# Matmul with layer norm: B loaded in half-width blocks that three row panels share, late gamma and beta, and a last panel computed quarter by quarter

## The chip, the cores and the metric

The kernel runs on one core of one Trainium2 chip. The metric is the device time of one execution in microseconds (us). The profile's span, from the first to the last instruction, is about 2 us shorter than the time. The *granted clock* is the share of PE's full clock that the profile shows as allowed.

Engines are called as the profile calls them: PE (matrix engine; "PEld" its weight loads), DVE (vector engine), ACT (scalar engine), POOL and SP (here they mostly issue transfers).

## The reference

```python
m, k, n = 2048, 2048, 2048          # a: m x k, b: k x n, all float32
x = np.matmul(a, b)
mean = np.mean(x, axis=-1, keepdims=True)
var = np.var(x, axis=-1, keepdims=True)
out = gamma * (x - mean) / np.sqrt(var + eps) + beta
```

The kernel computes the product in float16 with float32 sums. The cast happens in the load.

## The kernel before

The 2048 rows of A are 16 *panels* of 128 rows. A panel is loaded whole (1 MiB read), transposed by PE in 16 pieces (two groups of eight, each copied out of PSUM by ACT), and multiplied with the 16 row blocks of B (128 rows each, index `kt`). One panel's result is four *quarters* of 128 x 512, and each quarter fills one PSUM bank. Seven banks serve quarters, one serves transposes. A quarter takes 16 matmuls. Then DVE takes its statistics (`bn_stats`), ACT copies it to SBUF, and the bank is free. When all four are done, DVE makes two elementwise passes per quarter, and SP stores the panel.

```python
a16_lst[0] = emit_a_load(0)
a16_lst[1] = emit_a_load(1)
for kt in range(n_kt):                                   # B: 16 transfers of 1 MiB
    nc.gpsimd.dma_start(b16[:, kt, :], b[ts(kt, P), :])
at_lst[0] = emit_transposes(a16_lst[0], 0)
nc.sync.dma_start(gamma_b, gamma.unsqueeze(0).to_broadcast([P, N]))
nc.sync.dma_start(beta_b, beta.unsqueeze(0).to_broadcast([P, N]))
# ... [cut]
for i in range(n_mt):
    alloc_panel(i)                                       # four banks of seven
    for kt in range(n_kt):
        for q in range(n_nb):
            emit_mm(i, q, kt)
        if kt == n_kt // 2 - 1:
            # [cut] transposes of panel i+1, load of panel i+2
    x_sb_l[i] = [quarter_done(i, q) for q in range(n_nb)]   # bn_stats, copy
    emit_ln(i)                                              # 2 passes x 4 on DVE, stores
```

A scheduler reorders instructions at build time and the order on each engine is then fixed. It had moved three of panel 1's quarters up into panel 0, so that all seven banks were in use while B arrived.

## Time and profile before

| | |
|---|---|
| time | 284.34 us (4 runs, 284.25 to 284.39) |
| span of the profiled run | 282.4 us |
| first transpose | 10.3 us |
| B complete in PE's eyes | 53.2 us |
| last matmul ends | 270.7 us |
| PE busy | 87% of the span |

The timeline of PE before. Columns: start, duration, engine, source line, operation, output<-inputs, number of instructions, and in brackets the idle time before it with what ended it.

```profile
10.29 1.03 PE L76 MATMUL tps<-ident,a 128*128 128x128 f16 x8 [10.29 <-DMA a<-in_a_dram]
...
22.69 1.67 PE L107 MATMUL cps<-b,at 128*128 128x512 f16 x7 [0.85 <-DMA b<-in_b_dram]
...
53.20 1.67 PE L107 MATMUL cps<-b,at 128*128 128x512 f16 x7 [0.77 <-DMA b<-in_b_dram]
...
250.80 19.91 PE L107 MATMUL cps<-b,at 128*128 128x512 f16 x91
```

Seven matmuls (tps are transposes, cps quarters), a wait for B, seven matmuls: PE follows the loads until 53.2 us. After 64 us it has no listed gap, so it is the limit. The last line starts at 250.80 and lasts 19.91 us, so the last matmul ends at 270.71.

The waits of PE before (who waited for whom, us in total, times, longest):

```profile
PE cps L107 <- DMA b<-in_b_dram: 13.3, 15, 1.9
...
PE tps L76 <- DMA a<-in_a_dram: 11.0, 2, 10.3
```

The end of the chain of waits before, which follows the work that ended last (start, us, what; DVEq is DVE's sequencer):

```profile
250.97 19.12 PE cps L107 x88
270.08 0.02 issue
270.11 2.50 DVE bnst L116 x4
...
277.79 0.66 DVEq L189
```

Four bn_stats stand in the tail, then eight elementwise passes.

### The profile page before, as it was taken

How to read it: one execution, taken by the hardware profiler on the slowest of the kernel's cores; microseconds unless marked ns; L12 is line 12 of the kernel's file. 1: busy time of each engine (PE TensorE's matmuls, PEld its weight loads, DVE VectorE, ACT ScalarE, POOL GpSimd, SP SyncE). 2: the span in 40 equal slices, each digit the busy share in tenths (PEclk: the TensorE clock that was granted, in tenths of full speed). 3: DMA queues.
4: the chain of work that ended last, by engine and by line, in shares of the span. 5: the costliest groups of instructions: out<-in, count | busy, mean ns of one | idle time of the engine just before them, and what ended most of it. 6: DMA issues, size and time to landing. Idle time of an engine off the chain costs nothing.

```text
span 282.4 us, 3151 instructions
## 1 busy us (share of the span) xinstructions
PE 244.6 (87%) x1280; PEld 115.6 (41%) x1280; DVE 132.5 (47%) x241; ACT 73.9 (26%) x114; POOL 17.7 (6%) x38
## 2 busy tenths in 40 slices
PE   0286666699999999999999999999999999999930
PEld 0242222244444454545454545444444545454410
DVE  0000000389390919283645647382909092836474
ACT  1230000254232323232323232222323232323030
POOL 7122120000000000000000000000000000000000
PEclk9999999999999999999999999999999999999995
DMA  7999999967616160605243343425161203030303
GB/s 268 241 211 214 214 214 213 214 102 256 161 75 149 68 158 13 193 20 178 48 157 66 151 74 138 85 89 136 74 149 68 84 13 138 0 149 2 149 0 149
DMA packets 9517, 35.84 MB, mean 127 GB/s; under 512 B 1056, under 2 KB 1056, under 8 KB 9248
## 3 DMA queue, kind: packets, MB, share of 16 engines
q0 software_dynamic: 4608, 16.78, 31.6%
q1 hardware_dynamic: 4896, 18.88, 16.9%
q8 instruction: 10, 0.16, 0.2%
q14 instruction: 3, 0.02, 0.0%
HBM read 35.65 MB, written 16.78 MB: 186 GB/s over the span
## 4 chain that ended last, share of the span: by engine, by line
PE 73%; DMA 18%; DVE 5%; ACT 2%; issue 1%; POOL 0%; DVEq 0%; POOLq 0%
PE cps L107 68%; DMA b<-in_b_dram 14%; PE tps L76 5%; DMA a<-in_a_dram 4%; DVE c L139 2%; DVE u L135 2%; DVE bnst L116 1%; ACT x L118 1%; ACT L127 0%; DVEq L189 0%; POOL a L67 0%; DVE mv L123 0%; POOL ident masks.py:199 0%; ACT sq L127 0%; POOL ident masks.py:197 0%
## 5 line engine op out<-in xcount | busy, mean ns | idle before, releaser
L107 PE MATMUL cps<-b,at 128*128 128x512 f16 x1024 | 231.4, 380 | 13.6 <-DMA b<-in_b_dram 13.3
L107 PEld LDWEIGHTS <-at 128*128 128x128 f16 x1024 | 99.0, 98 | 131.7 <-issue 22.1
L116 DVE BATCH_NORM_STATS2 bnst<-cps 128x6 f32<-128x512 f32 x64 | 39.9, 685 | 143.1 <-PE cps L107 143.1
L118 ACT COPY x<-cps 128x512 f32<-128x512 f32 x64 | 37.4, 585 | 113.2 <-DVE bnst L116 112.3
L77 ACT COPY at<-tps 128x1024 f16<-128x1024 f16 x32 | 32.4, 1011 | 85.4 <-PE tps L76 85.4
L135 DVE SCALAR_TENSOR_TENSOR u<-x,mv,gamma_b 128x512 f32<-128x512 f32 x64 | 46.0, 742 | 0.0
L139 DVE SCALAR_TENSOR_TENSOR c<-u,rstd,beta_b 128x512 f32<-128x512 f32 x64 | 45.1, 745 | 0.0
L76 PE MATMUL tps<-ident,a 128*128 128x128 f16 x256 | 20.9, 227 | 12.6 <-DMA a<-in_a_dram 11.0
L76 PEld LDWEIGHTS <-a 128*128 128x128 f16 x256 | 17.9, 102 | 22.9 <-DMA a<-in_a_dram 11.5
L67 POOL DMA_DIRECT2D a<-in_a_dram x16 | 8.6, 538 | 166.4 <-PE tps L76 159.0
L86 POOL DMA_DIRECT2D b<-in_b_dram x16 | 8.5, 541 | 22.0 <-DMA b<-in_b_dram 15.5
L123 DVE BATCH_NORM_AGGREGATE mv<-bnst 128x2 f32<-128x24 f32 x16 | 4.2, 264 | 0.6
L127 ACT ACTIVATE sq<-ve 128x1 f32<-128x1 f32 x16 | 3.3, 207 | 0.0
L129 DVE RECIPROCAL rstd<-sq 128x1 f32<-128x1 f32 x16 | 2.5, 156 | 1.0 <-ACT sq L127 1.0
L125 DVE TENSOR_TENSOR ve<-mv,eps_t 128x1 f32<-128x1 f32 x16 | 2.5, 159 | 0.5
L77 ACT ACT_TABLE_LOAD x1 | 1.3, 1283 | 0.7 <-PEq L175 0.7
L127 ACT ACT_TABLE_LOAD x1 | 1.3, 1283 | 0.0
L93 DVE MEMSET eps_t<- 128x1 f32 x1 | 0.1, 59 | 0.8 <-PEq L175 0.8
masks.py:199 POOL TENSOR_SCALAR_AFFINE_SELECT ident<-ident 128x128 f16<-128x128 f16 x1 | 0.3, 304 | 0.1
masks.py:197 POOL MEMSET ident<- 128x128 f16 x1 | 0.2, 204 | 0.3 <-POOLq L175 0.3
L175 POOL MEMSET const-float32-0.0<- 128x1 f32 x1 | 0.1, 98 | 0.2 <-issue 0.2
L175 POOL MEMSET const-bfloat16-1.0<- 128x1 bf16 x1 | 0.1, 101 | 0.0
(2 smaller groups left out, 0.2 us busy)
## 6 DMA issues: line engine op xcount, KB each, us to landing
out_dram<-c SPq DMA_DIRECT2D x32, 512.0 KB, 2.6
a<-in_a_dram POOLq DMA_DIRECT2D x16, 512.0 KB, 5.1
b<-in_b_dram POOLq DMA_DIRECT2D x16, 512.0 KB, 19.8
gamma_b<-in_gamma_dram SPq DMA_DIRECT2D x1, 1024.0 KB, 4.5
beta_b<-in_beta_dram SPq DMA_DIRECT2D x1, 1024.0 KB, 8.8
```

Source lines behind the costliest of these rows:

```text
L67: nc.gpsimd.dma_start(a16, a[ts(i, P), :])
L76: nc.tensor.transpose(t_ps[:, j, :], a16[:, ts(h * 8 + j, P)], ident)
L77: nc.scalar.copy(at[:, ds(h * 8, 8), :], t_ps)
L86: nc.gpsimd.dma_start(b16[:, kt, :], b[ts(kt, P), :])
L107: nc.tensor.matmul(c_ps_l[i][q], at_lst[i][:, kt, :], b16[:, kt, ds(q * NB, NB)], start=(kt == 0), stop=(kt == n_kt - 1),)
L116: nc.vector.bn_stats(bnst_l[i][:, q, :], c_ps_l[i][q])
L118: nc.scalar.copy(x_sb, c_ps_l[i][q])
L123: nc.vector.bn_aggr(mv, bnst_l[i])
L125: nc.vector.tensor_tensor(ve, mv[:, 1:2], eps_t, AluOp.add)
L127: nc.scalar.activation(sq, ve, ActFn.Sqrt)
L135: nc.vector.scalar_tensor_tensor(u, x_sb_l[i][q], mv[:, 0:1], gamma_b[:, qs], AluOp.subtract, AluOp.mult,)
L139: nc.vector.scalar_tensor_tensor(c_sb[:, qs], u, rstd, beta_b[:, qs], AluOp.mult, AluOp.add,)
```

## The change

The intent is to give PE more work for every byte of B that has arrived, to start it earlier, and to shorten the tail.

```diff
-    for kt in range(n_kt):
-        nc.gpsimd.dma_start(b16[:, kt, :], b[ts(kt, P), :])
-    at_lst[0] = emit_transposes(a16_lst[0], 0)
-    nc.sync.dma_start(gamma_b, ...)          # and beta
+    NP = 3
+    HN = N // 2
+    at_lst[0] = emit_transposes(0)
+    load_b(0, 0)                             # load_b(h, kt): columns h*1024 to (h+1)*1024
+    load_b(0, 1)
+    a16_lst[2] = emit_a_load(2)
+    at_lst[1] = emit_transposes(1)
+    at_lst[2] = emit_transposes(2)
+    for kt in range(2, n_kt):
+        load_b(0, kt)
+    for kt in range(n_kt - 3):
+        load_b(1, kt)
+    a16_lst[3] = emit_a_load(3)
+    for kt in range(n_kt - 3, n_kt):
+        load_b(1, kt)
+    nc.gpsimd.dma_start(gamma_b, ...)        # and beta
+    a16_lst[4] = emit_a_load(4)
 ...
+    SK = 4
+    for h in range(2):                       # panels 0, 1, 2 together: six quarters per half
+        pairs = [(p, 2 * h + q) for p in range(NP) for q in range(2)]
+        # [cut] kt outer, pairs inner; in half 0 the last SK kt run pair by pair, each
+        # followed by quarter_done; in half 1 the first SK kt run pair by pair;
+        # panel 3's transposes near the end of half 1
+    for p in range(NP):
+        emit_ln_stats(p)
+    emit_ln_stt(0)                           # elementwise passes of panel 0
+    for i in range(NP, n_mt):
+        last = i == n_mt - 1
+        if last:
+            for q in range(n_nb):            # quarter by quarter
+                for kt in range(n_kt):
+                    emit_mm(i, q, kt)
+                quarter_done(i, q)
+        else:
+            # [cut] as before
+        emit_ln_stats(i)
+        if i - NP + 1 < NP:
+            emit_ln_stt(i - NP + 1)          # panel 1 with panel 3, panel 2 with panel 4
+        emit_ln_stt(i)
```

The pools are deeper as well (A 3 to 5, transposed A 2 to 5, copied quarters 6 to 20, results 2 to 3), which the three open panels need.

## The prediction

> **What bounds the kernel now.** Until 55.6 us, the loads: the timeline of PE shows bursts of 7 matmuls (1.67 us) separated by waits of 0.70 to 0.86 us on B, one burst per 2.44 us, so B's 1 MiB row blocks are read at about 430 GB/s. The Trainium skill ("DMA: Bandwidth & Descriptors", Specifications) gives 435 GB/s as the fabric ceiling; the trace agrees, so the loads cannot get faster. By 55.6 us PE has done only 112 of 1024 matmuls and 32 of 256 transposes. Then PE is the limit: 15.0 us per row panel (64 matmuls 0.216 us apart, 16 transposes adding about 1.2 us), without gaps, to 270.1 us. Then a tail of 12.3 us: four bn_stats (2.5), aggregation and square root, eight elementwise passes (5.3), output store (3.9). Span 282.4; the time is 1.9 above it.
>
> **What the change does.**
> 1. B comes as half blocks, and six quarters (three panels times two column blocks) use each. A half block should land every 1.22 us (an estimate, half of 2.44) and feeds 6 x 0.216 = 1.30 us of PE, so PE becomes the limit during B as well. Rows of 4 KB should move nearly as fast: the hardware queue's packets (mostly 4 KB) took about 0.156 us, the software queue's about 0.31 us for 8 KB read.
> 2. gamma and beta (2 MiB) leave the front of the transfers; A's first panel landed at 10.3 us behind them. Alone, an A panel lands 4.9 us after issue: at about 6.2 us.
> 3. The last panel runs quarter by quarter: three of four bn_stats leave the tail, 1.9 us saved.
> 4. Normalisation of panels 1 and 2 is delayed. DVE then owes two panels' elementwise work (10.6 us) plus 2.5 and about 1 in a 15 us panel: it just fits, with about 1 us of PE waiting for a PSUM bank at panel 4. Where the second half ends, six quarters finish together: at most 0.5 us more.
>
> **Sum.** The static order holds PE to the loads until the fourth half block: A0 6.2, A1 8.7, two half blocks 11.1, A2 13.6, half blocks 3 and 4 at 14.8 and 16.0 us. By 16.4 us it has done 8 matmuls and 24 transposes; the rest, 1016 x 0.216 + 232 x 0.074 = 236.5 us, runs nearly without gaps, the loads staying ahead (half 0: PE ends near 37 us, load near 31; half 1: 59 and 53). Last matmul: 252.9 + 1.5 bank waits + 0.5 slow first matmuls = 254.9. Tail 10.5. Span 265.4, time 267.3. 15 of the 17 us come from the critical path's first 55 us.
>
> **Predicted: 267 us, 80% range 262 to 272.** Faster by over 2%: 0.96; within 2%: 0.03; slower: 0.01.
>
> **What would show it.** First transpose near 6 us. PE's waits on B gone after about 17 us; PE share rising to about 93%. B's last half block near 53 us, PE at the second half's end near 59. Matmuls idle before an ACT copy of x: one or two waits, 1.5 us in all. Panels still 15.0 us apart. One bn_stats after the last matmul; last matmul near 255.
>
> **What would make it wrong.** Half blocks slower than 1.30 us (shorter rows, more issues on the Pool queue): each 0.1 us costs up to 3 us. DVE falling behind in panels 3 to 5, PE waiting for banks at several boundaries. A lower granted clock. The broadcast loads on the software queue delaying A4 and panel 4's transposes.

## The result, and the profile after

The changed kernel takes 267.9 us (median of 8 runs, 267.62 to 269.19), against 284.36 us for the kernel before (13 runs). The ratio is 0.9424, with a 95% interval of 0.9413 to 0.9435. A ratio is the mean time of one kernel's fast runs over the mean of the other's fast runs in the same rounds, so it is not quite the ratio of the medians. The span is 265.6 us, and the granted clock of both profiled runs is the same (0.987 and 0.986).

The timeline of PE after:

```profile
6.41 1.03 PE L77 MATMUL tps<-ident,a 128*128 128x128 f16 x8 [6.41 <-DMA a<-in_a_dram]
...
15.64 1.01 PE L128 MATMUL cps<-b,at 128*128 128x512 f16 x2 [1.78 <-DMA b<-in_b_dram]
16.93 1.01 PE L128 MATMUL cps<-b,at 128*128 128x512 f16 x2 [0.28 <-DMA b<-in_b_dram]
...
18.59 1.45 PE L128 MATMUL cps<-b,at 128*128 128x512 f16 x5
...
22.04 36.42 PE L128 MATMUL cps<-b,at 128*128 128x512 f16 x168
...
77.20 2.96 PE L128 MATMUL cps<-b,at 128*128 128x512 f16 x13 [0.59 <-ACT x L139]
...
235.66 19.80 PE L128 MATMUL cps<-b,at 128*128 128x512 f16 x91
```

PE starts at 6.41 us and waits for B for the last time at 16.93. From 22.04 us it runs 168 matmuls without a gap, while the loads are still going on. The only later wait is 0.59 us for a bank. The last matmul ends at 255.46 us, which is 15.25 us sooner than before.

The waits of PE after:

```profile
PE tps L77 <- DMA a<-in_a_dram: 6.4, 1, 6.4
...
PE cps L128 <- DMA b<-in_b_dram: 3.5, 4, 1.8
...
PE cps L128 <- ACT x L139: 0.6, 1, 0.6
```

The end of the chain of waits after:

```profile
235.82 19.66 PE cps L128 x91
...
255.50 0.71 DVE bnst L137
...
261.39 0.66 DVEq L255
```

One bn_stats is left in the tail. From the last matmul to the end of the span it is now 10.1 us (265.6 - 255.5), before it was 11.7 (282.4 - 270.7). So of the 16.8 us of span, 15.25 come from PE finishing earlier and about 1.55 from the tail.

### The profile page after: what moved, and what is told of

The parts are those of the page before. It is cut to its first block, busy times and chain, and to the rows that moved or that the text cites. A ratio compares the mean times of both kernels' runs of the same rounds, so it can differ in the third digit from the quotient of the medians.

```text
span 265.6 us, 3149 instructions
## 1 busy us (share of the span) xinstructions
PE 243.1 (92%) x1280; PEld 116.2 (44%) x1280; DVE 132.6 (50%) x242; ACT 73.6 (28%) x114; POOL 27.0 (10%) x55
## 4 chain that ended last, share of the span: by engine, by line
PE 79%; DVE 6%; ACT 6%; DMA 5%; POOL 1%; issue 1%; DVEq 0%; ACTq 0%; POOLq 0%
PE cps L128 74%; PE tps L77 5%; DMA b<-in_b_dram 5%; ACT at L78 4%; DVE c L165 3%; DVE u L161 3%; ACT x L139 1%; POOL a L64 1%; POOL b L97 1%; DVE bnst L137 1%; ACT L148 0%; DVEq L255 0%; DVE rstd L150 0%; POOL ident L84 0%; DVE mv L144 0%
## 5 line engine op out<-in xcount | busy, mean ns | idle before, releaser
L137 DVE BATCH_NORM_STATS2 bnst<-cps 128x6 f32<-128x512 f32 x64 | 40.5, 687 | 126.4 <-PE cps L128 126.4
L97 POOL DMA_DIRECT2D b<-in_b_dram x32 | 17.0, 534 | 24.3 <-DMA b<-in_b_dram 19.7
```

The costliest lines, as they stand in the source:

```text
L97: nc.gpsimd.dma_start(b16[:, kt, ds(h * HN, HN)], b[ts(kt, P), ds(h * HN, HN)])
L137: nc.vector.bn_stats(bnst_l[i][:, q, :], c_ps_l[i][q])
```

## The experiments

There were two theories of where the gain comes from. Theory T is the prediction's: six quarters per half block bring PE up to the pace of the loads, and the other parts are worth a few us at most. The rival R says that the earlier start earns most of it and the third panel little. Twelve kernels were run and all gave correct results. The kernel before, timed in the same rounds, took 284.4 to 284.6 us (medians). The changed kernel was timed in its own rounds only, so a difference from its 267.90 us is one between rounds, linked by the kernel before.

| run | what | median us | ratio to before |
|---|---|---|---|
| changed kernel | | 267.90 | 0.9424 |
| gb_front | gamma and beta first again | 272.35 | 0.9575 |
| np2 | two panels instead of three | 277.77 | 0.9771 |
| last_kt | last panel in the old order | 269.56 | 0.9479 |
| stt_now | normalisation not spread | 270.09 | 0.9511 |
| sk0 | no staggering of the halves | 268.58 | 0.9438 |
| b_gb_late | before, gamma and beta late | 280.35 | 0.9859 |
| b_last_q | before, last panel by quarters | 283.18 | 0.9958 |
| b_half | before, half-width loads | 285.23 | 1.0030 |
| ahalf | changed, half A panels | 267.56 | 0.9411 |
| warm | changed, dummy matmuls first | 268.97 | 0.9451 |
| best | ahalf and smaller last stores | 267.31 | 0.9397 |
| warm_best | best with dummy matmuls | 267.46 | 0.9402 |

### Undoing the late gamma and beta (gb_front)

```diff
+    nc.sync.dma_start(gamma_b, gamma.unsqueeze(0).to_broadcast([P, N]))
+    nc.sync.dma_start(beta_b, beta.unsqueeze(0).to_broadcast([P, N]))
     a16_lst[0] = emit_a_load(0)
 ...
-    nc.gpsimd.dma_start(gamma_b, ...)
-    nc.gpsimd.dma_start(beta_b, ...)
```

> The changed kernel with one part undone: gamma and beta are loaded first again, on the hardware queue, as in the kernel before. Theory T (six quarters per half block made PE the limit; the move of gamma and beta only shifts everything): all loads land 4 to 5 us later, first transpose near 10.3 us, PE without waits from about 21 us instead of 16.9, last matmul near 259.7, time about 272.3 us (271 to 273.5), so 4.4 of the 16.5 us. Rival R (the earlier start earns most of the gain, the third panel little): time 278 us or more.

It took 272.35 us, 4.4 more than the changed kernel. The timeline of PE in this run:

```profile
10.49 1.04 PE L77 MATMUL tps<-ident,a 128*128 128x128 f16 x8 [10.49 <-DMA a<-in_a_dram]
...
20.99 1.01 PE L128 MATMUL cps<-b,at 128*128 128x512 f16 x2 [0.22 <-DMA b<-in_b_dram]
...
27.13 36.42 PE L128 MATMUL cps<-b,at 128*128 128x512 f16 x168
```

The pattern of the changed kernel is there, about 4.1 us later up to the last wait for B. The 168 matmuls in a row start 5.1 us later in this profile; that start varies between runs (see warm). By the medians, the early start is worth about 4.4 of the 16.5 us. R asked for ten or more.

### Two panels instead of three (np2)

```diff
-    NP = 3
+    NP = 2
```

The third A panel is loaded where the fourth was, and the fourth where the fifth was.

> The changed kernel with two panels instead of three on each half block, everything else (gamma and beta late, last panel by quarters, half blocks, staggering) as changed. T: a half block then feeds only 4 x 0.216 = 0.86 us of PE per 1.25 to 1.33 us of load, so PE waits on B until the last half block at about 54 us (one A panel less in front of it than 56.5), having done 128 matmuls and 48 transposes by 55.3 us; the other 896 and 208 take 208.9 us, last matmul 264.2, tail 10.1, time about 276.6 us (275 to 278). R (half blocks and early start earn it): about 268 us, as the changed kernel.

It took 277.77 us, so the third panel is worth about 9.9 us, more than all the rest. R falls. The timeline of PE in this run:

```profile
27.91 0.38 PE L126 MATMUL cps<-b,at 128*128 128x512 f16 x1 [0.60 <-DMA b<-in_b_dram]
...
51.59 1.02 PE L126 MATMUL cps<-b,at 128*128 128x512 f16 x4 [2.71 <-DMA b<-in_b_dram]
52.83 1.44 PE L126 MATMUL cps<-b,at 128*128 128x512 f16 x4 [0.21 <-DMA b<-in_b_dram]
...
54.92 1.91 PE L126 MATMUL cps<-b,at 128*128 128x512 f16 x4
```

Its waits on B are 9.8 us in all, where the changed kernel has 3.5:

```profile
PE cps L126 <- DMA b<-in_b_dram: 9.8, 11, 2.7
```

PE waits for B up to 52.8 us, as T said. The run is 1.2 us slower than T's 276.6. The lines after the long wait of 2.71 us show why at least in part: at 54.92 us four matmuls take 1.91 us, where four at 0.216 us apart and 0.38 long take 1.03. The granted clock of this run is 0.57 from 53 to 57 us, and 0.90 from 24 to 58 us, against 1.00 in the changed kernel.

### Undoing the new last panel (last_kt), and doing it alone (b_last_q)

```diff
-        last = i == n_mt - 1
+        last = False
```

> The changed kernel with the last panel in the old order (all four quarters end together). T: the matmuls end as before at about 255.5 us, four bn_stats instead of one follow them, tail 11.9 instead of 10.1 us, time 269.7 us (+1.8). A null result (under 0.5) would say that the elementwise passes, not the bn_stats, set the tail.

In b_last_q the last panel of the kernel before runs quarter by quarter and nothing else changes.

> The kernel before with only its last panel computed quarter by quarter. T: one bn_stats instead of four after the last matmul: -1.8 us, 282.6 us, nothing else changed.

The first took 1.7 us more than the changed kernel, the second only 1.25 us less than the kernel before. The chain of waits in last_kt:

```profile
256.19 2.50 DVE bnst L137 x4
```

The four bn_stats are back in the tail. The size of 1.8 us was wrong, however. In the old order bn_stats of quarter 0 starts three matmuls (0.65 us) before PE is done, so the saving is 1.79 - 0.65 = about 1.15 us. That fits b_last_q: its last matmul ends at 270.79 us, next to 270.71 in the kernel before, and its span is 1.1 us shorter. The profiled run of last_kt is 2.5 us longer than that of the changed kernel: its tail is 1.2 us longer (11.3 against 10.1 us), as this sum has it, and PE ends 1.3 us later, because its full speed starts later, which the section on warm takes up.

### Normalising panels 0 to 2 at once (stt_now)

```diff
-    emit_ln_stt(0)
+    for p in range(NP):
+        emit_ln_stt(p)
 ...
-        if i - NP + 1 < NP:
-            emit_ln_stt(i - NP + 1)
```

> The changed kernel with the normalisation of panels 0, 1 and 2 all emitted at once after the second half, not spread over panels 3 and 4. T: DVE gets to panel 3's bn_stats 5.3 us later (about 81.2 instead of 75.9 us), the matmuls of panel 4's fourth quarter wait for its PSUM bank about 2.2 us instead of 0.6, and nothing later: time about +1.6 us, 269.5. If the delay were needless (slack in the banks), under 0.3 us.

It took 270.09 us (269.48 to 272.22), so the spreading is worth about 2 us. The profiled run was the one of 272.22 us. The timeline of PE in it:

```profile
71.12 9.88 PE L128 MATMUL cps<-b,at 128*128 128x512 f16 x45
83.07 4.85 PE L128 MATMUL cps<-b,at 128*128 128x512 f16 x14 [2.08 <-ACT x L139]
```

The wait for the bank is 2.08 us where the changed kernel has 0.59: T's 2.2 us. There is a second cost: the 14 matmuls after the wait take 4.85 us, where 14 at full speed take 3.2 (13 x 0.216 + 0.38). The profile's stretches show the clock in this run (stretch, length, busy us of PE, PEld, DVE, ACT and POOL, each with its count, then granted clock, DMA share, GB/s):

```profile
78.00:83.00 5.00, 2.99 (x14) 1.27 (x13) 5.00 (x9) 0.56 (x1) 0.00 (x0) 1.00 0.90 359
83.00:88.00 5.00, 4.93 (x19) 2.02 (x19) 4.93 (x12) 1.89 (x5) 0.00 (x0) 0.66 0.29 118
```

The granted clock fell to 0.66 on average after the wait. In this run the 168 matmuls in a row also start 1.4 us later than in the changed kernel (23.40 us), so its 4.6 us over the profiled run of the changed kernel are that, 1.5 us of wait and about 1.7 us of slow matmuls. The other three runs took 269.5 to 270.2 us. Their mean granted clock is 0.989 to 0.991, against 0.982 in this one, so they probably kept the clock up; their traces were not kept.

### No staggering between the halves (sk0)

```diff
-    SK = 4
+    SK = 0
```

> The changed kernel without the staggering between the two halves: all six quarters of half 0 end together. T: one bank is free and the others come free every 0.65 to 0.7 us from 1.3 us after the end on, while PE wants one every 0.65 us, so PE waits 0.3 to 1 us in all: 268.2 to 268.9 us. If the staggering is what keeps PE fed, several us more.

It took 268.58 us. The interval of its ratio (0.9425 to 0.9451) overlaps that of the changed kernel, so no difference is shown. (In the profiled run the 168 matmuls in a row start at 22.98 us, 0.9 us later than in the changed kernel's, which is nearly all of the 1.0 us between the two.) Its waits on PE are those of the changed kernel, with no wait for a bank at the seam between the halves:

```profile
PE cps L128 <- DMA b<-in_b_dram: 3.5, 4, 1.8
...
PE cps L128 <- ACT x L139: 0.6, 1, 0.6
```

The predicted 0.3 to 1 us of waits did not appear: with seven banks the seam needs no staggering.

### The kernel before with gamma and beta late (b_gb_late)

```diff
-    nc.sync.dma_start(gamma_b, ...)
-    nc.sync.dma_start(beta_b, ...)
+    a16_lst[2] = emit_a_load(2)
+    nc.gpsimd.dma_start(gamma_b, ...)
+    nc.gpsimd.dma_start(beta_b, ...)
```

> The kernel before with one part of the change alone: gamma and beta (and ahead of them the third A panel) are loaded after B, on the software queue. T: B's last row block lands 4 to 5 us earlier (about 48.8 instead of 53.2 us), but panel 0's elementwise passes now wait for beta until about 56 us, and the bn_stats of panel 1 stand behind them on DVE, so PE waits for a bank until about 61.7 us, where it came to that point at 64.3 us before: net -2.6 us, 281.8 us. If the late normalisation cost nothing: -4.4 us, 280.0.

It took 280.35 us, 4.1 less than before (4.7 less in the span), where T had said 2.6. The timeline of DVE in this run:

```profile
54.42 2.72 DVE L136 SCALAR_TENSOR_TENSOR u<-x,mv,gamma_b 128x512 f32<-128x512 f32 x4
57.06 0.69 DVE L117 BATCH_NORM_STATS2 bnst<-cps 128x6 f32<-128x512 f32 x1
57.66 2.73 DVE L140 SCALAR_TENSOR_TENSOR c<-u,rstd,beta_b 128x512 f32<-128x512 f32 x4
```

The scheduler put panel 1's first bn_stats between the passes, so the bank came free before PE wanted it and nothing was given back. The two ways of measuring this part agree: 4.4 us undone, 4.1 us alone.

### The kernel before with half-width loads (b_half)

```diff
-        nc.gpsimd.dma_start(b16[:, kt, :], b[ts(kt, P), :])
+        for h in range(2):
+            hs = ds(h * (N // 2), N // 2)
+            nc.gpsimd.dma_start(b16[:, kt, hs], b[ts(kt, P), hs])
```

> The kernel before with each row block of B loaded as two half-width transfers (rows of 4 KB instead of 8), order of the matmuls as before. T: shorter rows cost next to nothing: row blocks still arrive every 2.44 to 2.56 us, time 284.4 to 285.5 us. If half-width loads were themselves faster or slower, by 10 per cent either way, the time would be 4 us less or more.

It took 285.23 us, 0.3% more. Half-width blocks alone gain nothing and cost almost nothing; they are only what makes three panels fit into seven banks. The Trainium skill ("DMA: Bandwidth & Descriptors", Rules for kernel authors) asks for at least 1 MiB per transfer for the highest bandwidth. Here, with up to eight transfers in flight, halving loads of 1 MiB (bytes read; half as many are written, as float16) cost 0.8 us over the 16 MiB of B.

### Half A panels at the start (ahalf)

The first three A panels come as halves, so that six quarters can start after four half-size transfers.

```diff
-    a16_lst[0] = emit_a_load(0)              # and 1, 2
+    load_ah(0, 0); load_b(0, 0); load_ah(1, 0); load_ah(2, 0)
+    load_b(0, 1); load_b(0, 2); load_b(0, 3)
+    load_ah(0, 1); load_b(0, 4); load_ah(1, 1); load_b(0, 5); load_ah(2, 1)
+    # each half panel is transposed on its own; then as before
```

> The changed kernel with the first three A panels loaded as half panels between the first half blocks of B, so that six quarters can start after 2 MB instead of after 4 MB of loads. T: PE starts near 5.3 us and is without waits from about 11 us instead of 16.9, until it meets the loads: the last half block still lands near 56 us, so the second half ends near 58.5 instead of 60.7 us and the time is 265.4 us (-2.0 to -2.7). If the loads had slack to the end, -4.9: 263 us. If PE merely collects the waits later, no change.

It took 267.56 us: nothing worth naming. The timeline of PE in this run:

```profile
9.75 1.04 PE L94 MATMUL tps<-ident,a 128*128 128x128 f16 x8 [3.33 <-DMA a<-in_a_dram]
...
14.73 2.34 PE L154 MATMUL cps<-b,at 128*128 128x512 f16 x5
...
34.20 24.12 PE L154 MATMUL cps<-b,at 128*128 128x512 f16 x111 [0.62 <-DMA b<-in_b_dram]
```

Counting matmuls in the timelines up to 34.20 us gives 75 here. The changed kernel has done 18 before 22.04 us and then one every 0.216 us, so 74 by then. The early work is done in a cramped, slow way (five matmuls in 2.34 us), and at 34.2 us PE has caught up with the loads anyway. The wait at 34.20 us is for the last of the 11 MiB of the three panels and the first half of B. By its loops, the staggered order wants that last half block at matmul 76; without staggering, for which sk0 shows no need, it would be matmul 91. Half panels without staggering were not tried. My expectation had placed the limit of the loads at the end of the second half; it showed at the end of the first.

### Matmuls of zeros before the data (warm)

```diff
+    warm_z = konst.tile([P, NB], FP16)
+    nc.vector.memset(warm_z, 0.0)
+    warm_ps = psum.tile([P, NB], FP32, tag="c_ps", bufs=7)
+    for _ in range(14):
+        nc.tensor.matmul(warm_ps, warm_z[:, ds(0, P)], warm_z, start=True, stop=True)
```

> The changed kernel plus 14 matmuls of zeros into a spare PSUM bank while PE waits for the first A panel. In the changed kernel PE's first 16 transposes took 1.03 us per eight and its first matmuls were 0.43 us apart, against 0.61 and 0.216 later. Theory C (PE is slow until it has been busy for a few us without longer gaps, and the dummies end that before the data is there): first transposes 0.61 us per eight, the slow stretch is gone after the last wait for B (16.9 us), which takes about 1.2 to 1.6 us off: 266.5 us, and the runs spread less than 267.6 to 269.2. Rival D (the first instructions on real data are slow for another reason, or the slow stretch lies wholly in waits): no change, 267.9.

It took 268.97 us, 1.1 more than the changed kernel. The idea failed, and the profile shows how in part. The timeline of PE in this run:

```profile
1.19 4.74 PE L73 MATMUL warm_ps<-warm_z 128*128 128x512 f16 x14 [1.19 <-DVE warm_z L68]
6.43 0.62 PE L87 MATMUL tps<-ident,a 128*128 128x128 f16 x8 [0.49 <-DMA a<-in_a_dram]
8.15 0.61 PE L87 MATMUL tps<-ident,a 128*128 128x128 f16 x8 [1.10 <-ACT at L88]
10.12 0.59 PE L138 MATMUL cps<-b,at 128*128 128x512 f16 x2 [1.36 <-DMA b<-in_b_dram]
12.04 1.01 PE L138 MATMUL cps<-b,at 128*128 128x512 f16 x2 [1.33 <-DMA b<-in_b_dram]
...
23.26 36.42 PE L138 MATMUL cps<-b,at 128*128 128x512 f16 x168
```

The stretches of the same run (columns as above):

```profile
6.00:10.00 4.00, 1.23 (x16) 0.99 (x17) 0.00 (x0) 2.02 (x2) 1.06 (x2) 1.00 1.09 206
10.00:12.00 2.00, 0.59 (x2) 0.19 (x2) 0.00 (x0) 0.00 (x0) 0.53 (x1) 0.80 1.05 160
12.00:16.90 4.90, 2.87 (x12) 1.41 (x12) 0.00 (x0) 1.01 (x1) 1.59 (x3) 0.50 1.08 208
```

The zeros did bring PE up to speed: the first transposes take 0.62 us per eight, not 1.03. So theory C is right about the cause of the slow first work. But from 6 to 12 us PE is busy only 1.8 us, and the granted clock falls to 0.50, just before the work that counts. The Trainium skill ("TensorE: Matmul & The Clock Gate", Part 1) describes this: the clock of PE is halved by default, and about 3.4 us of sustained activity release it. The trace agrees on the halving: two matmuls take 0.59 us at 10.1 us, before the fall, and 1.01 us once the granted clock is 0.50. It fits the time too: the 14 matmuls of zeros take 4.74 us, which about seven gaps of 0.43 us and then gaps of 0.216 us make up, so full speed came after about 3.1 us (an estimate from these numbers). After the fall, full speed comes back later here than in the changed kernel's profile: the 168 matmuls in a row start at 23.26 us instead of 22.04. Why is not shown. That start moves between runs and variants without zeros as well: it is at 22.98 us in sk0, 23.26 in last_kt and 23.40 in stt_now. Five matmuls that start between 18.6 and 18.9 us take 1.45 us in the changed kernel's profile and 2.22 to 2.34 in these three. The profiled run of the changed kernel is the fastest of its eight. Its one run of 269.19 us may be such a late start, but its trace was not kept.

### Combining (best and warm_best)

best is ahalf with the fourth A panel in halves and the last panel stored in four pieces. warm_best adds 19 matmuls of zeros to that.

```diff
-    a16_lst[3] = emit_a_load(3)
+    load_ah(3, 0)                            # load_ah(3, 1) after B; transposed within panel 3
 ...
-        emit_ln_stt(i)
+        emit_ln_stt(i, 4 if last else 2)     # stores of the last panel
```

> The half-panel loads of the first three panels as in the run before, which moved nothing (267.56), with the fourth A panel loaded in halves too (the second after B) and the last panel stored in four pieces. T: the loads are not the limit at the end of the second half, so the first part gives nothing more; the last store is half as large, so the tail is 0.5 to 0.6 us shorter: 267.0 us.

> The same with 19 matmuls of zeros before the first transposes. C: with half panels PE worked on data from 9.8 us but slowly (matmuls 0.43 us apart until 17 us), which is why they gained nothing; warmed up, the gain shows: 2 to 3 us below the run without the zeros, 264.5 us. D: as without them.

best took 267.31 us, and its interval (0.9384 to 0.9410) lies just below that of the changed kernel: about 0.2 to 0.3% faster, across rounds. It is the fastest version tried by its median, but its interval overlaps those of ahalf and warm_best. It is not faster for the reason given: the profiled spans are both 265.6 us, PE ends at 255.0 us instead of 255.5, and the tail has grown to 10.6 us. The smaller last store took longer, not shorter: 4.0 us from the end of the chain's last DVE piece to the end of the span (261.6 to 265.6), against 3.55 us in the changed kernel. Why is open; keeping the two-piece store may be worth another half us, which was not tried. warm_best took 267.46 us, no better. The timeline of PE in warm_best:

```profile
16.10 0.62 PE L104 MATMUL tps<-ident,a 128*128 128x128 f16 x8 [1.03 <-DMA a<-in_a_dram]
...
18.54 0.62 PE L104 MATMUL tps<-ident,a 128*128 128x128 f16 x8 [0.74 <-DMA a<-in_a_dram]
...
21.11 0.62 PE L104 MATMUL tps<-ident,a 128*128 128x128 f16 x8 [0.87 <-DMA a<-in_a_dram]
...
34.25 24.12 PE L166 MATMUL cps<-b,at 128*128 128x512 f16 x111 [0.86 <-DMA b<-in_b_dram]
```

Now PE stays at full speed (granted clock 1.00 from 1 to 24 us), and the time it gains turns into waits for the loads. At 34.25 us it has the same 111 matmuls of that stretch ahead of it as ahalf had at 34.20. Speed of PE in the first 34 us is not the limit; the loads are, together with the order in which PE wants them. Whether another fixed order on PE, which would not wait for the second half panels so early, could turn those waits into work was not tried.

## Why the prediction was right, point by point

- **Time.** 267.0 was predicted, 267.9 measured, within the range. The mechanism held. That the number came so close was partly luck: the fourth half block was 0.9 us later than the sum had it, the waits for banks 0.9 us shorter, and the two cancelled.
- **First transpose near 6 us:** 6.41. **Waits on B gone after about 17 us:** the last is at 16.93. The sum had the fourth half block at 16.0.
- **The third panel is the core of the gain, the early start worth about 4 us.** np2 (9.9 us) and gb_front (4.4 us) show it.
- **Half blocks every 1.22 us.** Mis-sized. After the changed kernel's front, POOL's issues, each of which waits for a landing, come 1.20 to 1.33 us apart as a rule, with single gaps of 2.33, 1.82 and 1.47 us. The last half block landed near 56.5 us rather than 53 (an estimate: POOL saw the third from last land at 54.07 us, and two more follow at 1.25 each). PE was behind the loads by then, so this cost nothing. The second half ended near 60.8 us rather than 59: PE was late from the start, as above.
- **Bank waits of 1.5 us.** Mis-sized: 0.59 us in all. There was none where the second half ends, and stt_now shows that the spreading of the normalisation is what keeps it small.
- **0.5 us for slow first matmuls.** About 0.7: from 16.93 to 22.04 us PE did 12 matmuls and 24 transposes, worth 4.4 us at full speed, in 5.1 us. This term varies between runs, and the prediction did not see that.
- **1.9 us from the last panel.** About 1.15 us (b_last_q), because the first bn_stats had overlapped the last three matmuls. The 270.1 us that the prediction called the end of PE was the end of quarter 0; PE ended at 270.7. The last store was about 0.4 us shorter than before (from the end of the chain's last DVE piece to the end of the span, 3.55 against 3.95 us), which made up for part of it. Why is open: it is 3.94 us in b_last_q and 3.57 in last_kt, so the order of the last panel does not do it.
- **PE share 93%:** 92%. **Panels 15.0 us apart:** 15.02 (from 85.6 to 235.8 us in the chain, ten panels).
- **112 matmuls by 55.6 us before:** the trace has 107. Five matmuls are 1.1 us, and the sum did not use the count.
- **What holds the loads.** The prediction put 430 GB/s beside a ceiling of 435 and took it that the loads could not get faster. Its 430 are bytes read; the profile counts the bytes written, 213 GB/s while B arrives. From 55 to 57 us, when mostly gamma and beta arrived (no cast), the changed kernel wrote 424 GB/s. So writing into SBUF was not what held B back at 213. What does is not shown; in these runs row blocks came no faster than about 2.44 us apart as a rule.

## What to carry to other kernels

While a shared operand streams in as fast as its loads can go, count the work per arriving byte: PE had 7 x 0.216 = 1.5 us of work per 2.44 us of load, and 6 x 0.216 = 1.3 per half block after the change. Narrowing the block and widening the set of row panels that use it raised that within the same PSUM banks, and it earned more than everything else in the change together with little cost in bandwidth. Read the tail from what finishes last and not from the last matmul alone, and treat short waits of PE as possibly costing twice: once as the wait and once as slow matmuls after it.

## What the Trainium skill lacked or had wrong

- "TensorE: Matmul & The Clock Gate", Why this matters for your kernels: it advises no PE-idle gaps above about 3 us between bursts. That is too generous here. In the run warm the granted clock fell to 0.50 though no single wait exceeded 1.4 us; PE had been busy only 1.8 of 6 us. In the profiled run of stt_now one wait of 2.08 us was followed by a mean granted clock of 0.66 over 5 us. (Elsewhere the page does say that frequent short idle stretches bring the half clock back; the advice leaves them out.)
- "TensorE: Matmul & The Clock Gate" warns that the throttle's trace events can be unreliable, but no page says that the granted clock of a profile may be shown as 1.00 before its first change: in the changed kernel it is 1.00 from 6 to 17 us, while matmuls there are 0.43 us apart (two in 1.01 us).
- "DMA: Bandwidth & Descriptors", Rules for kernel authors: at least 1 MiB per transfer. It does not say what is lost with several in flight: with up to eight, halving to 512 KiB cost 0.8 us in 285 (b_half).
- No page explains the single late landings (gaps of 2.33 and 1.82 us between issues that otherwise come 1.20 to 1.33 us apart). What causes them stays open.
- No page says what limits a load that casts to half the bytes. Here B came at about 430 GB/s read (1 MiB per 2.44 us) and 213 written.
